# First MLP group's weights in GpSimd's queue, the last mixing product in another PSUM bank, and two tiles of activation sums exchanged

## The chip, the cores and the metric

The kernel runs on one core of one Trainium2 chip. A core has five engines, each with its own list of instructions that it works off in order: TensorE (PE in the profile; its weight loads are PEld), VectorE (DVE), ScalarE (ACT), GpSimd (POOL) and SyncE (SP). Engines wait for one another, and for transfers, by semaphores. Transfers are issued on a queue of the engine that issues them; here SP's queue is q1 in the profile and GpSimd's is q0, and 16 DMA engines carry both. The metric is device time in microseconds, the median of the runs shown.

## What is computed

A layer of a decoder with 512 tokens and width 2048, all in float32. The parts of the reference that matter here:

```python
merged = gc * conv_branch + ga * attn_branch
x = x + jnp.einsum('bsd,de->bse', merged, w_mix_out[l])

h = rmsnorm(x, g_mlp[l])
u = jnp.square(jax.nn.relu(jnp.einsum('bsd,df->bsf', h, w_ff1[l])))   # 2048 -> 8192
x = x + jnp.einsum('bsf,fd->bsd', u, w_ff2[l])                        # 8192 -> 2048
```

The three products are called mixing, FF1 and FF2 below.

## The kernel before

**Seven products for eight.** Every large product is cut in two along the tokens, the inner dimension and the output columns, and the eight quarter products are made from seven (the Winograd form of Strassen's scheme). A group makes 512 output columns. The seven activation operands are called A11, A12, A22 (quarters) and S1, S2, S3, S4 (sums and differences of quarters). Of the weights there are four quarters X[i, j], the tiles x00, x10, x01, x11 of 1024 KB each, 128 partitions by 8 runs of 256 floats; S1 takes x01 - x00, S2 takes x11 less that, S3 takes x11 - x01, A22 takes x10 less what S2 took. VectorE makes these differences (line 113). The profile leaves the numbers out: tile x is a weight quarter, A and S are operands.

**Three float32 passes.** TensorE multiplies rounded parts. Each weight tile is split into a high part th (ScalarE, line 103) and a rest tl (VectorE, line 104), each activation operand likewise, and a product is hi*hi + hi*lo + lo*hi: 48 matmuls of 256 columns, first the 32 that need th, then the 16 that need tl (in mixing, in two halves by token block, each with 16 and 8). Line 172, 173 and 175 are these three in mixing and FF2, lines 153, 155 and 157 in FF1; an `extra` in front (line 146) is one matmul of 192 columns. There are two buffers of th and of tl.

**Sums in PSUM.** A group adds its products in four PSUM banks a, b, c, d. ScalarE copies a bank into a tile o (`snap`, line 233), VectorE adds another bank to it (`plus`, line 116), and `put` hands a finished quarter of the output on.

**From mixing to the MLP.** Mixing has four groups g = 0 to 3, each a `Group` whose head runs A11 and A12 and whose tail runs the rest; the last uses `tail3` with the order S1, S2, S4, S3, A22. `Mix.put` adds the residual x (line 1111), stores the quarter into x1_d (line 1112) and leaves a `turn` in the list `waiting`. A turn squares the quarter for the norm (line 464), turns it by four TensorE transposes into a bank ptr (line 1128) and lets ScalarE write it with the gain into f (line 1137); the last group writes columns of Q2's A11 and A12 straight from ptr (lines 1133, 1134). From the two f tiles of a mixing group VectorE makes the sums s1, S2, S3, S4 of the next operand set Q2 (`first_of`, `sums`), and `give` splits them and sends them to h_d in HBM (line 1153). Shortly before FF1 the first three quarters of each Q2 operand come back from f_d (A11, A12; 768 KB, line 1088) and h_d (the others; 1536 KB each in runs of 6 KB, line 1086), all on GpSimd's queue, and the last mixing group adds the last quarter on chip (`mix.out`).

**Where the order comes from.** `Steps` attaches work to the moment after a product's matmuls have been written down, by the product's name: turns, `begin_part` (a load of a Q2 operand), `split_part` (A11's and A12's loaded columns). A scheduler then orders each engine's list by what it expects to be ready, except for instructions pinned with `keep_in_program_order` or `issue_after`. Weight tiles sit in four slots x0 to x3, handed out from the list `free`; a load waits for the last use of its slot's former tile. All weight quarters are loaded on SP's queue (line 208). The first MLP group g0 loads x00 and x10 in `head`, x01 in `first_sum`, x11 in `tail2`.

**From FF1 to FF2.** FF1's 16 groups store the activation sums of FF2 in s_d. For each of 8 segments `load_sums` brings them into four tiles us in slots t4, t1, t3, t2 by the table US (line 1331, 1 MB per transfer of two operands, GpSimd's queue). For the first segment these slots hold Q2 operands of FF1's last group: t1 holds S1, t3 holds S3, t4 A12, t2 A22. That group runs S4, S2, S3, S1, A22, so t3 falls free a product before t1. FF2's weights are the tiles y.

Of the kernel before, what the change touches and what calls it, by code (L numbers as in the profile page):

```python
# [45 lines left out]
def tile_hybrid_block(ctx: ExitStack, tc, x, g_mix, w_in, b_f, b_gate, conv_w, w_conv_out,  # L46
# [143 lines left out]
    class Group:  # L190
# [3 lines left out]
        def __init__(self, view, c1, c2, w, ST, mm, banks, put, scale=1.0, extra={}, after=None, shift=SHIFT):  # L194
# [3 lines left out]
            self.begun = False  # L198
# [3 lines left out]
        def load(self, i, j):  # L202
# [5 lines left out]
            nc.sync.dma_start(out=t, in_=src[i])  # L208
# [45 lines left out]

        def first(self):

            self.X = {}
# [6 lines left out]
        def head(self, keep=False, between=lambda: None, order=((0, 0), (1, 0)), rows=lambda i: None):  # L264
# [4 lines left out]
            else:  # L269
                X = self.X = {}  # L270
                for i, ij in enumerate(order):
                    X[ij] = self.load(*ij)
                    rows(i)
# [51 lines left out]
        def first_sum(self, pinned=True):  # L325

            self.pinned = True
            X = self.X
            X[0, 1] = self.load(0, 1)
# [41 lines left out]
        def tail3(self):  # L371
# [24 lines left out]
            self.run(d, "A22", X[1, 0], False)  # L396
            self.done(1, 0)
            self.plus(s2, d)
# [792 lines left out]
    before = None  # L1191
    mixes, groups = {}, []
    for g in range(4):
        def put_mix(i, j, v, g=g):
            mixes[g].put(i, j, v)

        banks = ((2,), (7,), (0,), (1,)) if g == 0 else steady(g)
        groups.append(Group(w_mix_out, g * S, g * S + HS, HS, M.moving, mm_rows if g else mm_late, banks, put_mix,
                            shift=48))
    for g in range(4):  # L1200
        mix = mixes[g] = Mix(g)
        after = Steps()
        if g == 0:
            for n, n2 in zip(("A11", "A12", "S1", "S3", "S2"), ("S1", "S3", "S2", "S4", "A22")):
                after.add(n, quads3[n2])
        if g == 3:
            after.add("S1", mix.fourth, lambda: begin_part("A12", 4))
        late = g == 1
        for n in ("A12", "S3") if late else ("A11", "S1"):
            after.add(n, turn_waiting)  # L1210
        after.add("A22", turn_first)
        if before:
            after.add("A12" if late else "A11", before.first_of, before.sums)
            for n, part in (("A12", "S1"), ("S1", "S3"), ("S2", "A22")):
                after.add(n, lambda before=before, part=part: before.give(part))
        if g < 3:
            after.add("S2", mix.fourth)
        else:
            after.add("A12", lambda: begin_part("A11", 0))
            after.add("S4", lambda: begin_part("S1", 1))  # L1220
# [5 lines left out]
        if g == 0:  # L1226
            after.add("A11", group.first_sum)
# [29 lines left out]

    held = []

    def put_u(g):
# [301 lines left out]
```

## Time and profile before

| | us |
|---|---|
| runs | 2448.61, 2451.72, 2453.45 |
| median | 2451.72 |
| the profiled execution | 2450.91 |
| its span, first to last instruction | 2449.2 |
| mixing's last group and the first MLP group | about 1156 to 1252 |
| FF1 ends, FF2 begins | 1825.3 |

In the timeline a row is a start, a duration, the engine, the line, the operation, and output<-input; brackets give the engine's idle time before the row and what ended it. A TensorE row's duration holds the pipeline's tail, so consecutive starts tell its pace better than durations.

### The profile page before, as it was taken

The page shows a single profiled execution, that of the slowest core. Times are in us where ns is not written, and L with a number is a line of the kernel's source. Part 1 is how long each engine was busy: PE and PEld are TensorE (multiplying, and loading weights), DVE is VectorE, ACT ScalarE, POOL GpSimd, SP SyncE. Part 2 cuts the span into 40 slices and gives each one's busy share as a digit, 9 for nine tenths or more (in the row PEclk, how much of TensorE's full clock was granted, in tenths as well). Part 3 has the DMA queues.
Part 4 walks back from the last instruction along what each step waited for, and adds up shares of the span by engine and source line. Part 5 has one row for each costly group of instructions (what it writes and reads, how often), then busy time and mean ns, then how long its engine had stood idle before and what let it go on. Part 6 is the DMA issues. An engine that isn't in the chain of part 4 may idle for free.

```text
span 2449.2 us, 41518 instructions
## 1 busy us (share of the span) xinstructions
PE 2409.1 (98%) x17800; PEld 2265.7 (93%) x17800; DVE 2041.6 (83%) x1717; ACT 1203.6 (49%) x1233; POOL 275.8 (11%) x442
## 2 busy tenths in 40 slices
PE   8999999999999999999899999999999999999998
PEld 8999899999999999899899999999997888888886
DVE  7987777788887778888889898898978888889898
ACT  6443434345455535356556666666655333333334
POOL 0100000111121111022300000000011001100000
PEclk9999999999999999999999999999999999999999
DMA  7664544454656655657854655646587476655662
GB/s 250 184 192 143 155 132 145 138 161 164 211 171 214 217 196 179 215 161 246 309 181 176 228 194 200 236 176 229 198 304 271 167 246 228 236 191 183 245 225 101
DMA packets 286988, 489.87 MB, mean 200 GB/s; under 512 B 11772, under 2 KB 199284, under 8 KB 286420
## 3 DMA queue, kind: packets, MB, share of 16 engines
q1 hardware_dynamic: 237072, 283.20, 36.6%
q0 software_dynamic: 48864, 202.92, 22.3%
q8 instruction: 139, 2.28, 0.4%
q10 hardware_dynamic: 868, 1.10, 0.1%
q14 instruction: 45, 0.37, 0.0%
HBM read 377.60 MB, written 109.05 MB: 199 GB/s over the span
## 4 chain that ended last, share of the span: by engine, by line
PE 90%; DVE 4%; DMA 3%; issue 2%; ACT 1%; POOL 1%; SPq 0%; DVEq 0%; POOLq 0%; ACTq 0%
PE a L157 6%; PE a L153 6%; PE a L155 6%; PE a L173 5%; PE a L175 5%; PE a L172 5%; PE d L153 5%; PE d L155 5%; PE d L157 5%; PE c L153 4%; PE c L155 4%; PE c L157 4%; PE d L172 3%; PE d L175 3%; PE d L173 3%; PE b L155 3%
## 5 line engine op out<-in xcount | busy, mean ns | idle before, releaser
L103 ACT ACTIVATE th<-x 128x2048 fp32r<-128x2048 f32 (+1 forms) x280 | 537.0, 1918 | 509.2 <-DVE x L113 169.5
L104 DVE TENSOR_TENSOR tl<-x,th 128x2048 fp32r<-128x2048 f32 (+1 forms) x280 | 638.8, 2286 | 166.6 <-ACT th L103 151.6
L113 DVE TENSOR_TENSOR x<-x,x 128x2048 f32<-128x2048 f32 (+1 forms) x160 | 365.6, 2285 | 28.6 <-DMA x<-in_w_in_dram 16.9
L103 ACT ACTIVATE th<-y 128x2048 fp32r<-128x2048 f32 (+1 forms) x109 | 185.4, 1701 | 273.1 <-PE a L173 138.8
L104 DVE TENSOR_TENSOR tl<-y,th 128x2048 fp32r<-128x2048 f32 (+1 forms) x109 | 218.9, 2013 | 28.9 <-ACT th L103 28.4
L172 PE MATMUL a<-th,us 128*128 128x512 f32 x512 | 199.9, 390 | 2.2 <-ACT th L103 2.2
L153 PE MATMUL c<-S,th 128*128 128x256 f32 x848 | 197.6, 278 | 2.5 <-ACT th L103 2.5
L173 PE MATMUL a<-th,us 128*128 128x512 f32 x512 | 199.8, 390 | 0.0
L155 PE MATMUL c<-S,th 128*128 128x256 f32 x848 | 197.0, 277 | 0.0
L153 PE MATMUL a<-S,th 128*128 128x256 f32 x784 | 182.6, 278 | 0.8 <-ACT th L103 0.8
L155 PE MATMUL a<-S,th 128*128 128x256 f32 x784 | 181.1, 276 | 0.0
L153 PEld LDWEIGHTS c<-S,th 128*128 128x128 f32 x848 | 159.8, 188 | 3.0 <-ACT th L103 2.7
L155 PEld LDWEIGHTS c<-S,th 128*128 128x128 f32 x848 | 159.7, 188 | 0.0
L153 PEld LDWEIGHTS a<-S,th 128*128 128x128 f32 x784 | 147.3, 188 | 1.0 <-ACT th L103 1.0
L155 PEld LDWEIGHTS a<-S,th 128*128 128x128 f32 x784 | 147.3, 188 | 0.0
L175 PE MATMUL a<-tl,us 128*128 128x512 f32 x512 | 137.5, 391 | 0.0
L155 PE MATMUL b<-A,th 128*128 128x256 f32 x544 | 128.4, 280 | 0.4 <-DVE A L104 0.4
L153 PE MATMUL b<-A,th 128*128 128x256 f32 x544 | 128.2, 280 | 0.0
L153 PE MATMUL d<-S,th 128*128 128x256 f32 x544 | 126.3, 278 | 0.0
L153 PE MATMUL a<-A,th 128*128 128x256 f32 x544 | 126.1, 277 | 0.0
L155 PE MATMUL a<-A,th 128*128 128x256 f32 x544 | 126.0, 277 | 0.0
L155 PE MATMUL d<-S,th 128*128 128x256 f32 x544 | 125.8, 277 | 0.0
(386 smaller groups left out, 6058.7 us busy)
## 6 DMA issues: line engine op xcount, KB each, us to landing
x<-in_w_in_dram SPq DMA_DIRECT2D x86, 1024.0 KB, 6.0
x<-in_w_ff_dram SPq DMA_DIRECT2D x64, 1024.0 KB, 8.4
y<-in_w_ff_dram SPq DMA_DIRECT2D x64, 1024.0 KB, 7.8
us<-s_d POOLq DMA_DIRECT2D x48, 1024.0 KB, 9.2
s_d<-rh POOLq DMA_DIRECT2D x32, 896.0 KB, 5.5
s_d<-r POOLq DMA_DIRECT2D x32, 896.0 KB, 6.1
x<-in_w_mix_out_dram SPq DMA_DIRECT2D x17, 1024.0 KB, 6.7
g_d<-o POOLq DMA_DIRECT2D x32, 256.0 KB, 3.0
```

The costliest lines, as they stand in the source:

```text
L103: a = nc.scalar.activation(out=hi, in_=src, func=AF.Copy, scale=one)
L104: b = nc.vector.tensor_tensor(out=lo, in0=src, in1=hi.bitcast(F32), op=ALU.subtract)
L113: return nc.vector.tensor_tensor(out=out, in0=a, in1=b, op=ALU.subtract)
L153: nc.tensor.matmul(o, hi[:, q, js], Sh, start=first and q == 0 and j == 0, stop=False, skip_group_check=True)
L155: nc.tensor.matmul(o, hi[:, q, js], Sl, start=False, stop=False, skip_group_check=True)
L157: nc.tensor.matmul(o, lo[:, q, js], Sh, start=False, stop=q == nq - 1, skip_group_check=True)
L172: nc.tensor.matmul(o, Sh, hi[:, q, :], start=begin and q == 0, stop=False, skip_group_check=True)
L173: nc.tensor.matmul(o, Sl, hi[:, q, :], start=False, stop=False, skip_group_check=True)
L175: nc.tensor.matmul(o, Sh, lo[:, q, :], start=False, stop=q == nq - 1, skip_group_check=True)
```

## The change

Three edits. First, `Group` gets a queue, and g0's is GpSimd's; the four quarters of g0 are loaded by a new method `ahead`, which is attached to the last mixing group's steps S4 (x00), S3 (x10) and A22 (x01) and to g0's own A11 (x11). `head`, `first_sum` and `tail2` then load only what is not there yet. For this the setup of the mixing groups moves, unchanged otherwise, behind the definition of `put_u`, `ff1` and g0. Second, in `tail3` the last product A22 starts anew in bank a instead of adding to d; d is added to s2 before, by a `plus` of its own. With it the turns of the last group that waited behind S1 wait behind S2. Third, in US the slots of (S2, S3) and (S1, A22) are exchanged.

```diff
-            self.begun = False
+            self.begun, self.queue, self.X = False, nc.sync, {}
...
-            nc.sync.dma_start(out=t, in_=src[i])
+            self.queue.dma_start(out=t, in_=src[i])
...
+        def ahead(self, i, j):
+
+            self.X[i, j] = self.load(i, j)
+
...
         def first(self):
 
-            self.X = {}
             self.X[0, 0] = self.load(0, 0)
...
-                X = self.X = {}
+                X = self.X
                 for i, ij in enumerate(order):
-                    X[ij] = self.load(*ij)
+                    if ij not in self.at:
+                        X[ij] = self.load(*ij)
                     rows(i)
...
         def first_sum(self, pinned=True):
 
             self.pinned = True
-            X = self.X
-            X[0, 1] = self.load(0, 1)
+            X = self.quarters((0, 1))
             one = sub(X[0, 0], X[0, 1], X[0, 0])
...
             self.put(1, 1, d1)
-            self.run(d, "A22", X[1, 0], False)
+            self.plus(s2, d)
+            self.run(a, "A22", X[1, 0], True)
             self.done(1, 0)
-            self.plus(s2, d)
+            self.plus(s2, a)
             self.put(1, 0, s2)
...
     g0 = ff1(0, ((5,), (0,), (1,), (7,)))
-    g0.after = Steps(A11=[turn_waiting, begin_rest, lambda: first_sum_after(mix.added), mix.first_of],
+    g0.queue = nc.gpsimd
...
+        for n in ("A12", "S3") if late else ("A11", "S2" if g == 3 else "S1"):
             after.add(n, turn_waiting)
...
             after.add("A12", lambda: begin_part("A11", 0))
-            after.add("S4", lambda: begin_part("S1", 1))
+            after.add("S4", lambda: g0.ahead(0, 0), lambda: begin_part("S1", 1))
             after.add("S4", lambda: split_part("A11"))
-            after.add("S3", lambda: begin_part("S3", 3))
+            after.add("S3", lambda: g0.ahead(1, 0), lambda: begin_part("S3", 3))
+            after.add("A22", lambda: g0.ahead(0, 1))
             after.add("A22", lambda: split_part("A12"))
...
+    g0.after = Steps(A11=[lambda: g0.ahead(1, 1), turn_waiting, begin_rest, lambda: first_sum_after(mix.added), mix.first_of],
                      A12=[lambda: mix.out("S1", mix.s1), mix.sums, lambda: factors(common, turned)])
...
-    US = ((4, ("A11", "A12")), (1, ("S2", "S3")), (3, ("S1", "A22")), (2, ("S4",)))
+    US = ((4, ("A11", "A12")), (3, ("S2", "S3")), (1, ("S1", "A22")), (2, ("S4",)))
```

The scheduler orders the engines' lists anew around these places. GpSimd's list from the last store of a rest into h_d to the load of A22, before (numbers behind a name are the program's own for a buffer):

```order
L1153 DMA h_d_76<-f_11978 128x512 x2
L1086 DMA S1_12831<-h_d_76 128x2x1536
L1112 DMA x1_d_78<-o_12836 128x2x256
L1086 DMA S3_12894<-h_d_76 128x2x1536
L1112 DMA x1_d_78<-o_12716 128x2x256
L1112 DMA x1_d_78<-o_12776 128x2x256
L1086 DMA S2_13052<-h_d_76 128x2x1536
L1086 DMA S4_13054<-h_d_76 128x2x1536
L1086 DMA A22_13056<-h_d_76 128x2x1536
```

and now:

```order
L208 DMA x00_12833<-in_w_ff1_dram 128x8x256
L208 DMA x10_12898<-in_w_ff1_dram 128x8x256
L1157 DMA h_d_76<-staged_12772 128x512
L1157 DMA h_d_76<-f_11980 128x512
L1090 DMA S1_12835<-h_d_76 128x2x1536
L1116 DMA x1_d_78<-o_12840 128x2x256
L1090 DMA S3_12900<-h_d_76 128x2x1536
L1116 DMA x1_d_78<-o_12703 128x2x256
L208 DMA x01_12984<-in_w_ff1_dram 128x8x256
L1116 DMA x1_d_78<-o_12778 128x2x256
L208 DMA x11_13044<-in_w_ff1_dram 128x8x256
L1090 DMA S2_13057<-h_d_76 128x2x1536
```

x00 and x10 stand ahead of the second staged pair (a high part and its rest) and of S1, x01 before the last store, x11 behind it and ahead of S2, S4 and A22.

TensorE at the end of S1 (bank c) in the last mixing group, before:

```order
L175 MATMUL c_12638<-tl_12640,M_10796 128x256 x2
L175 MATMUL c_12638<-tl_12640,M_10996 128x256 x2
L1128 MATMUL ptr_12699<-ident_90,o_12564 128x128 x4
L172 MATMUL a_12472<-th_12718,M_10549 128x256
L173 MATMUL a_12472<-th_12718,M_10549 128x256
```

and now at the end of S2 (bank a):

```order
L175 MATMUL a_12474<-tl_12706,M_10796 128x256 x2
L175 MATMUL a_12474<-tl_12706,M_10996 128x256 x2
L1132 MATMUL ptr_12761<-ident_90,o_12566 128x128 x4
L173 MATMUL c_12640<-th_12781,M_10549 128x256
L172 MATMUL c_12640<-th_12781,M_10549 128x256
```

The four transposes (in one row) moved from the start of S2 to its end; one matmul of S4 now stands in front of S2's first tl.

VectorE behind the last mixing store and around the first MLP group's S1 (x00 becomes x01 - x00, s1 is made from the last turn, S1 and A22 are the rests of split operands), before:

```order
L113 TENSOR_TENSOR x00_12984<-x01_13058,x00_12984 128x2048
L104 TENSOR_TENSOR tl_13067<-x10_12986,th_13066 128x2048
L104 TENSOR_TENSOR A12_12693<-A12_12693 128x1536
L1245 TENSOR_REDUCE ms_13124<-ss2_11038 128x4
L104 TENSOR_TENSOR tl_13156<-x00_12984,th_13155 128x2048
L116 TENSOR_TENSOR s1_13061<-f_12465 128x512
L104 TENSOR_TENSOR A22_13056<-f_12465,A22_13056 128x512
L113 TENSOR_TENSOR f_12465<-f_12464,f_12465 128x512
L104 TENSOR_TENSOR S1_12831<-s1_13061,S1_12831 128x512
L113 TENSOR_TENSOR f_12464<-s1_13061,f_12464 128x512
```

and now:

```order
L104 TENSOR_TENSOR A22_13061<-f_12467,A22_13061 128x512
L113 TENSOR_TENSOR x00_12833<-x01_12984,x00_12833 128x2048
L104 TENSOR_TENSOR S1_12835<-s1_13064,S1_12835 128x512
L113 TENSOR_TENSOR f_12467<-f_12466,f_12467 128x512
L113 TENSOR_TENSOR f_12466<-s1_13064,f_12466 128x512
L1310 TENSOR_REDUCE mean_13134<-mean_13132 128x1
L113 TENSOR_TENSOR f_12466<-f_12466 128x512
L116 TENSOR_TENSOR o_13066<-b_13068,o_13066 128x512
L104 TENSOR_TENSOR S3_12900<-f_12467,S3_12900 128x512
L104 TENSOR_TENSOR S2_13057<-f_12466,S2_13057 128x512
L104 TENSOR_TENSOR S4_13059<-f_12466,S4_13059 128x512
L104 TENSOR_TENSOR tl_13157<-x00_12833,th_13156 128x2048
```

The difference x01 - x00 moved behind s1 (now one row ahead of the piece) and A22's rest, and the split of its result moved from in front of s1 to behind the rests of S3, S2 and S4.

117 lines of the change are left out of this document (58 added, 59 removed).

## The prediction

> **What bounds the kernel now.** The page's head comes first.
>
> ```profile
> span 2449.2 us, 41518 instructions
> PE 2409.1 (98%) x17800; PEld 2265.7 (93%) x17800; DVE 2041.6 (83%) x1717; ACT 1203.6 (49%) x1233; POOL 275.8 (11%) x442
> ```
>
> TensorE stands still for 40.1 us of the span. Only such gaps, and slow stretches behind them, can be won. I then listed TensorE in order of time around the two places that the diff touches. First the seam from mixing to the MLP (in brackets: idle time before the row, and what ended it):
>
> ```profile
> 1174.91 0.63 PE L1128 MATMUL ptr<-ident,o 128*128 128x128 f32 x4 [0.78 <-DVE o L1111]
> ...
> 1178.22 1.18 PE L175 MATMUL a<-tl,M 128*128 128x256 f32 x8 [0.86 <-DVE tl L104]
> ...
> 1193.88 0.36 PE L172 MATMUL d<-th,M 128*128 128x256 f32 x1 [0.88 <-DVE o L116]
> ...
> 1205.78 0.60 PE L1128 MATMUL ptr<-ident,o 128*128 128x128 f32 x4
> 1209.15 0.36 PE L146 MATMUL b<-A,th 128*128 128x192 f32 x1 [2.78 <-ACT A L103]
> ...
> 1212.19 0.58 PE L153 MATMUL c<-S,th 128*128 128x256 f32 x1 [2.54 <-ACT th L103]
> ...
> 1238.58 2.05 PE L157 MATMUL a<-S,tl 128*128 128x256 f32 x16
> ```
>
> The two long waits open the first MLP group's A12 and S1. The windows (TensorE's busy time first; the last three figures are granted clock, DMA share and GB/s) show a second price behind them:
>
> ```profile
> 1209.00:1212.00 3.00, 0.49 (x2) 0.30 (x2) 3.00 (x2) 2.27 (x4) 0.00 (x0) 0.93 1.02 402
> 1212.00:1215.00 3.00, 2.38 (x9) 2.09 (x10) 3.00 (x4) 2.26 (x7) 0.81 (x1) 0.50 1.03 411
> ```
>
> From 1212 the clock is halved, and the DMA engines are full at some 400 GB/s. Now the engines TensorE waited for:
>
> ```profile
> 1203.57 1.92 ACT L103 ACTIVATE th<-x 128x2048 fp32r<-128x2048 f32 x1 [4.73 <-DMA x<-in_w_ff_dram]
> ```
>
> ```profile
> 1207.84 2.29 DVE L113 TENSOR_TENSOR x<-x,x 128x2048 f32<-128x2048 f32 x1 [6.34 <-DMA x<-in_w_ff_dram]
> ...
> 1214.02 2.28 DVE L104 TENSOR_TENSOR tl<-x,th 128x2048 fp32r<-128x2048 f32 x1
> 1216.22 0.68 DVE L116 TENSOR_TENSOR s<-f 128x512 f32<-128x512 f32 x1
> 1216.82 0.68 DVE L104 TENSOR_TENSOR A<-f,A 128x512 fp32r<-128x512 f32 x1
> ```
>
> ScalarE stood 4.73 us until weight quarter x10 had landed, with A12's operand split queued behind, which is the ACT A that ended the 2.78; VectorE stood 6.34 us for x01. So at this seam the bound is the landing of two weight quarters. Why they are late: the DMA view gives the issues from 1178 to 1212 (size, median us to landing), and the queues from 1194 to 1196 (packets, MB, share of 16 engines):
>
> ```profile
> x<-in_w_ff_dram SPq DMA_DIRECT2D x4, 1024.0 KB, 22.1
> ```
>
> ```profile
> q0 software_dynamic: 112, 0.69, 84.2%
> q1 hardware_dynamic: 113, 0.11, 16.2%
> ```
>
> SP's queue (q1) and GpSimd's (q0) get equal packets, but a packet of an operand load is 6 KB and one of a weight quarter 1 KB. The weights get 0.11 MB of each 0.80 and take 22.1 us.
>
> **The change part by part.** *Weights in GpSimd's queue.* One queue serves its loads in the order of issue, so x00 and x10 no longer share with S1 and S3, and x01 follows S3. When do they land? GpSimd's queue is empty of older work by about this issue:
>
> ```profile
> 1179.78 0.54 POOL L1088 DMA_DIRECT2D A<-f_d  x1
> ```
>
> From there (sizes from the code) x10 ends a list of 1.83 MB of older transfers (four of 0.26 and A12's load, 0.79) and 2.10 MB of weights: 9.8 us at 400 GB/s, 1190. x01 has 9.16 MB up to its end (those 3.93, the staged pair 0.52, S1 and S3 3.15, two stores 0.52, itself 1.05): 22.9 us, 1203; with up to 2 us until the semaphore, 1205. Four issues more on GpSimd; the nearest row is
>
> ```profile
> L1331 POOL DMA_DIRECT2D us<-s_d x64 | 47.9, 752 | 369.8 <-PE b L175 218.0 <-PE d L175 105.1 <-PE a L175 26.9
> ```
>
> 0.75 us for 512 runs of 2 KB. A quarter has 1024 runs of 1 KB; between 0.75 and twice that I take 0.8, 3.2 us in all on an engine 11% busy. Behind x00 stand the second staged pair and S1, behind x01 a store and x11: all have microseconds to spare. SP loses four issues that nobody waits for.
>
> *A22 in bank a.* The 0.88 us before 1193.88 goes: bank a was read out before S3. The price is one more VectorE addition, 0.60 us (start to start of the 0.68 rows above), between additions that wait for S3 anyway: nothing.
>
> *Transposes after S2 instead of S1.* S2 still waits for tl, which VectorE makes at the same time:
>
> ```profile
> 1175.89 2.28 DVE L104 TENSOR_TENSOR tl<-x,th 128x2048 fp32r<-128x2048 f32 x1
> ```
>
> So S2 begins at 1174.0, where the wait before the transposes of 1174.91 began, runs its first 16 matmuls, stands until 1178.2 and ends as before; the four transposes, which lay in idle time, now cost about 0.4. Together with the line above, A11 starts 0.9 - 0.2 = 0.7 earlier, if tl holds S2 exactly as now.
>
> *The new path behind A11.* A11 ends near 1204.9, transposes 1205.2. A12's hi and lo parts are made by then, since x10 is there by 1192 and ScalarE's buffer free by 1198, so A12 runs 1205.6 to 1211.1 without its 2.78. The last turn's copies on ScalarE end at 1206.2. From there VectorE's new list is followed at 0.60 for 512 columns and 2.20 for 2048 (starts of the three rows from 1214.02): s1, A22's lo (1207.5), x01-x00 (1209.7), S1's lo and two sums (1211.5), then mean, which needs A12's end, five of 512 (1214.7), S1's tl (1216.9), S3's difference (1219.1), S3's tl after ScalarE's 1.9 (1223.2), S2's difference (1225.4). TensorE: S1 from 1211.6, its 32 hi matmuls 3.6 us, then 1.6 idle for tl, end 1218.8; S3 from 1221.0 (2.2 idle) to 1226.5; S2 from 1227.4 to 1232.9. Before, S2 ended at 1238.58 + 1.9 = 1240.5. **The sum is -7.6 us**, about VectorE's 6.34 us plus the 0.7; S4 and all after it are paced by TensorE (the chain of waits, the last part of each product):
>
> ```profile
> 1267.01 1.88 PE c L157 x16
> 1272.66 1.81 PE a L157 x16
> 1278.10 1.81 PE d L157 x16
> ```
>
> A product takes 5.65 us up to 1268 and 5.44 later. From 1240.5 five slow ones may become fast: 0 to -1.05; I take 0, as new gaps lie ahead of them too.
>
> *Places of S2,S3 and S1,A22 swapped.* At the seam from FF1 to FF2:
>
> ```profile
> 1814.91 1.52 POOL L1331 DMA_DIRECT2D us<-s_d  x2 [0.48 <-PE d L157]
> 1820.35 1.49 POOL L1331 DMA_DIRECT2D us<-s_d  x2 [3.92 <-PE a L157]
> ```
>
> ```profile
> 1834.32 2.29 DVE L113 TENSOR_TENSOR t<-y,y 128x2048 f32<-128x2048 f32 x1 [1.14 <-DMA y<-in_w_ff_dram]
> ```
>
> ```profile
> 1838.67 0.50 PE L172 MATMUL a<-th,us 128*128 128x512 f32 x1 [2.20 <-ACT th L103]
> ```
>
> ```profile
> us<-s_d POOLq DMA_DIRECT2D x2, 1024.0 KB, 15.4
> ```
>
> The tile freed first (1814.91) now takes S2,S3, 5.4 us earlier. But the pair issued at 1820.35 had landed, 15.4 us by the median, near 1837, before 1838.67; what came last was the weight difference t, begun at 1834.32. Same bytes, same issue times: 0. If the sums were the bound instead, up to -2.2.
>
> **The rivals.** *Half clock in the new gaps.* S2 of the last mixing group now stands 2.3 us in one piece, and S3 2.2. For the price there is
>
> ```profile
> 1838.00:1843.00 5.00, 4.33 (x12) 3.17 (x13) 5.00 (x3) 4.49 (x4) 0.56 (x1) 0.66 0.34 137
> ```
>
> after the single gap of 2.20: a third of 5 us, 1.7. Against it: the window behind the 2.78 gap shows 0.93, and 0.50 came only after a second gap. At S2 it costs 1.7, at S3 0.8, since 0.9 lies in S2's wait: -5.9 to -5.1, 2445.8 to 2446.6. [...]
>
> *The queue changes nothing.* The engines were full anyway, and x01 lands as late as now; left are the 0.7: 2451.0. For it: the same bytes must move from 1180 on. Against it: 22.1 us came from the 0.11 of 0.80 MB, and what is loaded ahead instead (S2, S4, A22) is needed later. [...]
>
> *Slower: the queue starves S1.* S1, S3, x00, x10 and nine smaller transfers now stand ahead of x01 in one queue, much of it in runs of 1 KB. From 1182 to 1184, when almost only weight packets moved, the answer was
>
> ```profile
> DMA packets 438, 0.47 MB, mean 237 GB/s; under 512 B 2, under 2 KB 429, under 8 KB 438
> ```
>
> At 237 GB/s the 9.16 MB take 38.6 us; x01 is there at 1220.6, 13.1 after VectorE wants it (1207.5): 13.1 - 7.6 = +5.5, 2457.2. It decides from 277 GB/s downward. Against it stand later 2 us of almost nothing but weights:
>
> ```profile
> q1 hardware_dynamic: 718, 0.72, 106.8%
> ```
>
> that is 360 GB/s. *Partly late*: at 320 GB/s x01 is 3.1 late, -4.5, 2447.2. [...]
>
> **How the numbers follow.** The profiled run took 2450.91 us, 1.7 more than its span, and lies 0.8 under the median of three, 2451.72. With -7.6 on the median: 2444.1. Chances: forecast 0.50, half clock 0.15, partly late 0.13, queue without effect 0.11, starved 0.11. The likeliest's own range is 2441.5 to 2446.5. The whole: down to -7.6 - 1.05 - 1.7 (no half clock at the second seam) = -10.4, taken as 2440.8, up to 2451.5, past the case without effect. What a measurement can tell is 0.2%, 4.9 us: faster below 2446.8, slower above 2456.6. Faster: nearly all of the forecast, most of the half clock, a third of the partly late: 0.65; slower 0.10; same 0.25.
>
> **What would show it.** ScalarE's th<-x for x10 and VectorE's x01-x00 without a DMA behind them; A12 within 0.5 us of the transposes; idle times of some 1.6, 2.2 and 0.9 before S1's tl, S3 and S2; no gap before A22; S2's end at the second seam unmoved against the landing of y. Wrong it would be if x01 still ends VectorE's wait, if weights in q0 take over 10 us from their turn, or if S2 of the last mixing group ends later than now.

## The result, and the profile after

| | before | changed |
|---|---|---|
| median of the runs compared, us | 2453.72 (20 runs, 2448.31 to 2459.63) | 2445.68 (20 runs, 2440.90 to 2449.22) |
| ratio, 95% interval | | 0.9964 (0.9956 to 0.9973) |
| the profiled execution, us | 2450.91 | 2446.44 |

The change makes the kernel 0.36% faster, 8.8 us by the ratio (6.6 to 10.8). The two profiled executions differ by 4.5 us only: the one of before lies 2.8 us under the median of its kernel, the one of the change 0.8 above its own.

The head of the page of the changed kernel:

```profile
span 2444.7 us, 41518 instructions
PE 2408.0 (98%) x17800; PEld 2265.2 (93%) x17800; DVE 2042.6 (84%) x1718; ACT 1203.9 (49%) x1233; POOL 277.9 (11%) x446
```

TensorE stands for 36.7 us of the span, before 40.1. Its timeline at the first seam (start, duration, engine, line, operation; in brackets the idle time and what ended it), from the last mixing group's S2 on:

```profile
1178.16 0.39 PE L172 MATMUL c<-th,M 128*128 128x256 f32 x1 [2.23 <-ACT o L233]
...
1193.37 0.28 PE L172 MATMUL a<-th,M 128*128 128x256 f32 x1
...
1205.17 0.60 PE L1132 MATMUL ptr<-ident,o 128*128 128x128 f32 x4
...
1212.29 0.39 PE L153 MATMUL c<-S,th 128*128 128x256 f32 x1 [0.60 <-ACT th L103]
...
1217.61 2.15 PE L157 MATMUL c<-S,tl 128*128 128x256 f32 x16 [1.41 <-DVE tl L104]
1221.81 0.53 PE L146 MATMUL d<-S,th 128*128 128x192 f32 x1 [2.05 <-ACT th L103]
...
1232.94 2.05 PE L157 MATMUL a<-S,tl 128*128 128x256 f32 x16
```

A22 follows at 1193.37 without a gap; A12 follows the transposes of 1205.17 without the 2.78 us. S2 stands 2.23 us in one piece. S1 and S3 of the first MLP group come within 0.8 us of the forecast, up to 1221.81, and S2's last part starts at 1232.94 where before it started at 1238.58. ScalarE and VectorE on the way there:

```profile
1192.66 1.92 ACT L103 ACTIVATE th<-x 128x2048 fp32r<-128x2048 f32 x1 [0.97 <-PE d L173]
...
1198.57 1.92 ACT L103 ACTIVATE th<-x 128x2048 fp32r<-128x2048 f32 x1
```

```profile
1206.73 0.69 DVE L116 TENSOR_TENSOR s<-f 128x512 f32<-128x512 f32 x1 [0.72 <-ACT f L1141]
...
1208.01 2.28 DVE L113 TENSOR_TENSOR x<-x,x 128x2048 f32<-128x2048 f32 x1
...
1215.27 2.28 DVE L104 TENSOR_TENSOR tl<-x,th 128x2048 fp32r<-128x2048 f32 x1
1217.47 2.29 DVE L113 TENSOR_TENSOR x<-x,x 128x2048 f32<-128x2048 f32 x1
1221.79 2.29 DVE L104 TENSOR_TENSOR tl<-x,th 128x2048 fp32r<-128x2048 f32 x1 [2.04 <-ACT th L103]
```

Neither th of x10 (1198.57) nor x01-x00 (1208.01) has a transfer behind it now. From 1206.73 VectorE works without a pause until 1219.76, and S1's tl and S3's difference are the end of that list: VectorE has taken the place of the transfers. The windows here are laid on the grid on which the granted clock changes (TensorE's busy time first, the granted clock third from the end):

```profile
1214.88:1218.29 3.41, 2.00 (x17) 1.81 (x16) 3.41 (x3) 0.00 (x0) 0.00 (x0) 1.00 1.03 422
1218.29:1221.71 3.42, 1.47 (x13) 1.26 (x11) 1.47 (x1) 1.86 (x2) 0.00 (x0) 1.00 0.70 286
1221.71:1225.12 3.41, 3.31 (x15) 3.31 (x16) 3.33 (x3) 1.29 (x3) 0.00 (x0) 0.50 0.04 14
```

One stretch of 3.41 us at half clock (from 1221.71) follows S3's wait of 2.05 us and costs 1.7 us. Before there were two at this seam (6.83 us from 1211.5) and one at the second seam; there the changed kernel has none. In the DMA view from 1178 to 1212 the weights now read:

```profile
q0 software_dynamic: 2808, 11.98, 95.8%
...
x<-in_w_ff_dram POOLq DMA_DIRECT2D x4, 1024.0 KB, 10.2
```

That is 10.2 us from issue to landing instead of 22.1. The figure alone says little: x01 was issued 12.5 us later than before (1198.10 against 1185.65) and landed at the same time.

### The profile page after: what moved, and what is told of

Same layout as the page of the kernel before. It is cut to its first block, busy times and chain, and to the rows that moved or that the text cites. A ratio compares the mean times of both kernels' runs of the same rounds, so it can differ in the third digit from the quotient of the medians.

```text
span 2444.7 us, 41518 instructions
## 1 busy us (share of the span) xinstructions
PE 2408.0 (98%) x17800; PEld 2265.2 (93%) x17800; DVE 2042.6 (84%) x1718; ACT 1203.9 (49%) x1233; POOL 277.9 (11%) x446
## 4 chain that ended last, share of the span: by engine, by line
PE 90%; DVE 4%; issue 2%; DMA 2%; ACT 1%; POOL 1%; SPq 0%; DVEq 0%; POOLq 0%; ACTq 0%
PE a L157 6%; PE a L153 6%; PE a L155 6%; PE a L175 5%; PE a L173 5%; PE a L172 5%; PE d L153 5%; PE d L155 5%; PE d L157 5%; PE c L153 4%; PE c L155 4%; PE c L157 4%; PE d L175 3%; PE d L173 3%; PE d L172 3%; PE b L153 3%
## 5 line engine op out<-in xcount | busy, mean ns | idle before, releaser
L113 DVE TENSOR_TENSOR x<-x,x 128x2048 f32<-128x2048 f32 (+1 forms) x160 | 366.1, 2288 | 21.2 <-DMA x<-in_w_in_dram 17.1
```

Source lines behind the costliest of these rows:

```text
L113: return nc.vector.tensor_tensor(out=out, in0=a, in1=b, op=ALU.subtract)
```

## The experiments

Each kernel was timed beside the kernel before on the same chip; a ratio's interval is turned into us at 2453 us. Places are counted from the start of the last mixing group's S1, since that start shifts by up to 4.0 us from one profile to the next (1168.04 to 1172.01). A product's end is counted as the start of the next one.

**The parts by themselves.** First the queue alone: the changed kernel with these three places put back.

```diff
+            self.run(d, "A22", X[1, 0], False)
+            self.done(1, 0)
             self.plus(s2, d)
-            self.run(a, "A22", X[1, 0], True)
-            self.done(1, 0)
-            self.plus(s2, a)
...
-        for n in ("A12", "S3") if late else ("A11", "S2" if g == 3 else "S1"):
+        for n in ("A12", "S3") if late else ("A11", "S1"):
...
-    US = ((4, ("A11", "A12")), (3, ("S2", "S3")), (1, ("S1", "A22")), (2, ("S4",)))
+    US = ((4, ("A11", "A12")), (1, ("S2", "S3")), (3, ("S1", "A22")), (2, ("S4",)))
```

> The first edit alone: the weights of the first MLP group in GpSimd's queue; the last mixing product stays in bank d, the turns stay behind S1, the places of the sums stay as they were. Theory (all of the gain comes from the first edit, the others together give at most 0.7 us): -7 us against before, between -5.5 and -8.5, and the end of the first MLP group's S2 near 1235.5 where before has 1240.5 and the whole change 1234.8. Rival (bank, turns and exchanged sums carry a part): -5 us or less.

Measured: ratio 0.9975 (0.9961 to 0.9989), -6.1 us (-9.6 to -2.7); S2 ended at 1236.08. The figure lies in the range of the theory, but the interval holds the rival's -5 as well. In the profile the queue alone carries 4 of the 5.6 us at this seam. It still shows 1.45 and 1.30 us of waits in A12, because in this list x10's load stood behind S1's and landed at 1200.7.

The other two edits, each alone on the kernel before:

```diff
-            self.run(d, "A22", X[1, 0], False)
+            self.plus(s2, d)
+            self.run(a, "A22", X[1, 0], True)
             self.done(1, 0)
-            self.plus(s2, d)
+            self.plus(s2, a)
...
-        for n in ("A12", "S3") if late else ("A11", "S1"):
+        for n in ("A12", "S3") if late else ("A11", "S2" if g == 3 else "S1"):
```

> The second edit alone: the last mixing product in bank a, and the turns of the last mixing group behind S2. Theory: the gap before A22 goes, S2 keeps its stall, TensorE's idle time from the last mixing group's S1 to the end of the first MLP group's S2 falls from 10.2 to about 9.3 us; at most -1 us against before, apart from half-clock stretches. Rival (the bank or the turns carry the 4 us by which the run with loads on SP lay under before): -3 us or more.

```diff
-    US = ((4, ("A11", "A12")), (1, ("S2", "S3")), (3, ("S1", "A22")), (2, ("S4",)))
+    US = ((4, ("A11", "A12")), (3, ("S2", "S3")), (1, ("S1", "A22")), (2, ("S4",)))
```

> The third edit alone: the places of (S2, S3) and (S1, A22) exchanged. Theory: 0 within the error, TensorE's wait for S2 at the second seam stays between 0.8 and 2.7 us and ends with the weight difference, not with the sums. Rival (the sums were the bound): -2.2 us, and no wait there.

Measured: bank and turns 0.9986 (0.9975 to 0.9998), -3.4 us (-6.1 to -0.5); the exchanged sums 1.0000 (0.9988 to 1.0011). So the exchange is worth nothing, as forecast; S2 of the second seam waited 1.67 us for th there, behind a weight difference that had waited 1.15 for y. Bank and turns are worth something; the interval holds the forecast 0.7 near its edge, and the -3.4 itself is the rival's figure. Both profiles were a surprise. VectorE and TensorE of the kernel with bank and turns alone, at the first seam:

```profile
1213.90 2.29 DVE L113 TENSOR_TENSOR x<-x,x 128x2048 f32<-128x2048 f32 x1 [11.26 <-DMA x<-in_w_ff_dram]
```

```profile
1218.25 0.58 PE L153 MATMUL c<-S,th 128*128 128x256 f32 x1 [10.50 <-ACT th L103]
```

With the weights still on SP's queue x01 came 4 us later than in the first profile of before, and TensorE stood 10.5 us in one piece. The two edits touch neither the queue nor the issue of that load (17.1 us behind S1's start in both). Idle time from S1 to S2's end was 15.2 us, not the expected 9.3. The same profile shows what bank and turns are worth beyond the forecast: x10 landed 6.2 us earlier than before, and the wait of 2.78 us before A12 is gone. With the turns behind S2, GpSimd issued no transfer between 13.3 and 20.2 us behind S1's start, where before it issued four stores from 16.2 on and S1's load at 19.8.

Then everything but the queue:

```diff
-    g0.queue = nc.gpsimd
```

> The whole change, but the four weight quarters stay on SP's queue; their loads are written at the new places. So it holds the second and the third edit without the first. VectorE's list keeps x01-x00 ahead of A12's rest, as before. Theory (the second and third edit give next to nothing): -0.4 us against before, between -1.0 and +0.3; A11 starts some 0.6 earlier, ScalarE again stands some 4 to 5 us for x10, VectorE some 6 us for x01, S2 of the first MLP group ends near 1240. Rival (writing the loads earlier is what counts, or the exchanged sums): -3 us or more.

Measured: 0.9983 (0.9967 to 1.0), -4.2 us (-8.1 to 0), with runs from 2441.65 to 2461.26. That is the rival's figure, not the theory's, though the interval reaches 0. x10 and x01 came early in its profile (1195.94, 1206.96), so ScalarE did not stand for x10, VectorE stood 3.58 us for x01 and S2 ended at 1240.53. Here too the scatter is larger than what was to be measured.

**Queue or list?** x01 landed at 1207.81 before and at 1207.79 after: in that pair the queue had not brought it forward. What had changed as well is VectorE's list: before, x01-x00 stands ahead of A12's rest, s1 and the sums, afterwards behind. The next two kernels are meant to separate the two. The list of the change with SP's queue:

```diff
-    g0.queue = nc.gpsimd
...
-            add(self.s1, self.F[1][:, 0], self.F[1][:, 1])
+            self.s1_add = nc.vector.tensor_tensor(out=self.s1, in0=self.F[1][:, 0], in1=self.F[1][:, 1], op=ALU.add)
...
-    g0.after = Steps(A11=[lambda: g0.ahead(1, 1), turn_waiting, begin_rest, lambda: first_sum_after(mix.added), mix.first_of],
+    g0.after = Steps(A11=[lambda: g0.ahead(1, 1), turn_waiting, begin_rest, mix.first_of, lambda: first_sum_after(mix.s1_add)],
```

> As the run with all loads on SP, but VectorE's difference x01-x00 is put behind s1 in its list, where the change has it, so that it no longer stands in front of A12's rest. The landings stay those of SP's queue: x10 near 1203.5, x01 near 1207.8. In the changed kernel x01 landed at 1207.79, in the kernel before at 1207.81, so the queue brought only x10 and x11 earlier. Theory of the landing (x10's 8.5 us earlier are what pays): A12 still waits for x10 and its operand split on ScalarE, -2 us or less against before, S2's end at 1238 or later. Rival, theory of the list (what paid is that VectorE does A12's rest, s1 and the sums while x01 is still on its way): A12 near 1211 to 1217, S3's th near 1221, S2's end near 1235, -4.5 to -6 us against before.

And GpSimd's queue with the old list (`behind` stands for a dependency of order only):

```diff
-            split(src, hi, lo)
+            rest = split(src, hi, lo)[1]
+            if n == "A12" and self.queue is nc.gpsimd:
+                behind(rest, self.one)
...
-            one = sub(X[0, 0], X[0, 1], X[0, 0])
+            one = self.one = sub(X[0, 0], X[0, 1], X[0, 0])
...
-            add(self.s1, self.F[1][:, 0], self.F[1][:, 1])
+            ins = nc.vector.tensor_tensor(out=self.s1, in0=self.F[1][:, 0], in1=self.F[1][:, 1], op=ALU.add)
+            if self.last:
+                behind(ins, g0.one)
```

> The whole change with GpSimd's queue, but in VectorE's list s1 and A12's rest are held behind x01-x00, as in the kernel before. x01 lands near 1207.8, x10 near 1195. Theory of the landing: A12 starts at 1205.5 and stands some 3 us before its tl, yet most of the gain stays, -5 us against before. Theory of the list: VectorE stands until 1207.8 and has some 5 us of work behind that in the change was done before or meanwhile; S1's rest begins near 1218 to 1220 where the change has 1215.3, S2's end 2.5 to 4 us later than the change's 1234.8, -1.5 to -4 us against before.

Measured: the list of the change on SP's queue 0.9989 (0.9976 to 1.0002), -2.7 us (-5.9 to +0.5), and S2 ended at 1239.82; the queue with the old list 0.9978 (0.9967 to 0.9989), -5.4 us (-8.1 to -2.7), S2's end 2.9 us later than in the change when counted from S1. On SP's queue with that list TensorE's two waits read:

```profile
1214.32 0.38 PE L153 MATMUL c<-S,th 128*128 128x256 f32 x1 [2.76 <-ACT th L103]
1225.97 0.53 PE L146 MATMUL d<-S,th 128*128 128x192 f32 x1 [4.32 <-ACT th L103]
```

and VectorE's reasons for them:

```profile
1210.03 2.29 DVE L113 TENSOR_TENSOR x<-x,x 128x2048 f32<-128x2048 f32 x1 [2.73 <-DMA x<-in_w_ff_dram]
...
1221.63 2.29 DVE L113 TENSOR_TENSOR x<-x,x 128x2048 f32<-128x2048 f32 x1 [1.35 <-DMA x<-in_w_ff_dram]
```

Where the list no longer stands in the way, S1 waits for x01 and S3 for x11 (landed at 1221.60; 1212.24 in the change). So the theory of the list fell: S2's end and the time miss what it expected, and the interval includes 0. A premise of that run did not hold either: x10 landed at 1194.86 on SP's queue too, not near 1203.5, and A12 did not wait. This bought little: S4 ended 76.26 us behind S1, before at 77.59 and 76.46. The theory of the landing got its -5 us for the queue with the old list, but not the profile: S1's rest began at 1220.51 and S2's end came as late as the list's theory had it. By the profiles the change needs both: its S4 ends at 72.0 and 72.5 us behind S1, that of the queue with the old list at 74.8, that of the list on SP's queue at 76.3, that of neither at 75.0. The runs give -8.8 us for both, -5.4 for the queue alone, -2.7 for the list alone and -4.2 for neither (everything but the queue, above); the last three intervals overlap, and these times do not separate the queue from the list. All four kernels hold the other two edits as well.

**The same kernels again.**

> The kernel before once more, for a second profile of it. Theory (with the weights on SP's queue the landings of x10 and x01 scatter from one execution to the next, and the first profile of before was an early one): x01 lands anywhere between 36 and 45 us behind the start of the last mixing group's S1 (39.3 in the first profile), and the later it lands the longer TensorE stands and the more half-clock stretches follow. Rival (the first profile is typical, the landing fixed): 39.3 within 0.5, idle time from that S1 to the end of the first MLP group's S2 10.2 within 0.5. On the clock: in all profiles so far a stretch of 3.41 us in which TensorE stood for 1.88 us or more was followed by one at half clock, and one with at most 1.76 was not; the same is expected here.

> The changed kernel once more, for a second profile of it. Theory (one queue serves in order, so the landings hardly scatter): x01 lands 38.9 to 40.1 us behind the start of the last mixing group's S1, as in the three profiles with GpSimd's queue, idle time to the end of S2 6 to 7 us, the time -6 to -10 us against before. Rival: x01's landing moves by 3 us or more here too.

Measured: before against itself 1.0003 (0.9987 to 1.0019); the change 0.9971 (0.9959 to 0.9984). The profiles so far together (us behind the start of the last mixing group's S1; idle is TensorE's, to the end of the first MLP group's S2; half-clock stretches and the last column to the end of S4):

| kernel | x10 lands | x01 lands | idle | half-clock stretches | S4 ends |
|---|---|---|---|---|---|
| before | 34.95 | 39.28 | 10.18 | 2 | 77.59 |
| before, again | 34.87 | 39.54 | 10.28 | 2 | 76.46 |
| sums exchanged alone | 33.46 | 44.43 | 14.95 | 4 | 82.52 |
| bank and turns alone | 28.71 | 43.50 | 15.20 | 4 | 81.48 |
| all but the queue | 24.94 | 35.96 | 9.32 | 1 | 74.97 |
| SP's queue, new list | 25.86 | 41.01 | 8.85 | 3 | 76.26 |
| GpSimd's queue, old list | 25.07 | 38.90 | 7.79 | 2 | 74.83 |
| queue alone | 32.66 | 40.05 | 6.81 | 2 | 73.48 |
| the change | 26.46 | 39.28 | 6.29 | 1 | 71.96 |
| the change, again | 26.50 | 39.92 | 6.96 | 1 | 72.47 |

The second profile of before, taken by itself, came out as the rival had it: x01 at 39.54, within 0.5 of 39.28, and the idle time at 10.28. What speaks for the scatter is the kernel with the exchanged sums alone. Its code is that of before except for a table used at the second seam, and its x01, issued at the same place, landed at 44.43. Over all six profiles with SP's queue x01 lands from 36.0 to 44.4, over the four with GpSimd's from 38.9 to 40.1; these are profiles of five and three kernels.

x10's landing does not follow the queue. It is early, 24.9 to 28.7, in all kernels in which the turns wait behind S2, with either queue, and late, 32.7 to 35.0, in all in which they wait behind S1. What follows the queue is x11: it lands 52.6 to 54.6 us behind S1 in the six profiles with SP's queue and 42.4 to 43.7 in the four with GpSimd's. In the change VectorE begins S3's difference, which needs x11, 49.0 us behind S1, before x11 would have landed on SP's queue.

The two profiles of before have times in the lower half of their kernel's: 2450.91 and 2448.03, where 12 runs of it have a median of 2454.30. Between them and the two of the change the seam, to S4's end, shrinks by 4.8 us on average (77.0 to 72.2). Over the five profiles with SP's queue and the old list it takes 78.6 us, 6.4 more than in the change, but three of these are of other kernels. The granted clock that every run lists shows another part. It averages 0.9960 over 78 runs of before and 0.9979 over 29 of the change; (1 - clock) times 2450 us is 9.7 and 5.2 us lost. By that estimate about half of the 8.8 us is half-clock time that no longer arises, and the rest would be waits that are gone.

**The next bound.** In the change VectorE's list runs from 1206.73 to 1219.76 without a pause. First only x01 earlier: its load ahead of S3's operand, and x01-x00 right behind A12's rest.

```diff
             self.done(0, 1)
+            self.freed()
...
-            after.add("S3", lambda: g0.ahead(1, 0), lambda: begin_part("S3", 3))
-            after.add("A22", lambda: g0.ahead(0, 1))
+            after.add("S3", lambda: g0.ahead(1, 0))
...
+        group.freed = lambda: (g0.ahead(0, 1), begin_part("S3", 3))
...
-    g0.after = Steps(A11=[lambda: g0.ahead(1, 1), turn_waiting, begin_rest, lambda: first_sum_after(mix.added), mix.first_of],
+    g0.after = Steps(A11=[lambda: g0.ahead(1, 1), turn_waiting, begin_rest, lambda: first_sum_after(part_rest["A12"]), mix.first_of],
```

`part_rest["A12"]` is the instruction on VectorE that makes the rest of A12's loaded columns.

> The whole change, with x01's load issued as soon as its slot is free, ahead of the load of S3's operand, and x01-x00 put right behind A12's operand rest on VectorE. Theory (behind A12 VectorE's own list is the bound, not the landing any more): x01 lands near 1203.3 instead of 1207.8, VectorE does x01-x00 from about 1206, and S3's difference x11-x01 ends 1.0 to 1.5 us earlier than in the changed kernel, because tl of S1 still stands behind the rests of S3, S2, S4; S2's end some 1.2 us earlier, the time -1 to -2 us against the changed kernel. Rival (the landing of x01 is still the bound): -4 us or more against the changed kernel.

Then, on top, S1's rest and S3's difference ahead of the operand rests of S3, S2, S4 and A22:

```diff
+            self.third(third)
...
-            sub(X[two], X[1, 1], X[0, 0])
+            self.two(sub(X[two], X[1, 1], X[0, 0]))
...
-    for n in SPLIT[1:]:
-        mix.out(n, mix.parts[n])
+    def rest_of(ins, *names):
+        with tc.issue_after(ins.ins):
+            for n in names:
+                mix.out(n, mix.parts[n])
...
+    g0.third = lambda ins: rest_of(ins, "S3")
+    g0.two = behind
```

with `behind` calling `rest_of` for S2, S4 and A22.

> As the run with x01's load early, and on VectorE the rest of S1's weights and S3's weight difference go ahead of the operand rests of S3, S2, S4 and A22. Theory (VectorE's list is the bound behind A12): TensorE's gaps before S1's tl, S3 and S2 shrink from 2.0, 2.05 and 0 (with a half-clock stretch of 1.7 between) to 0, at most 0.5 and some 0.9, none long enough for the clock to halve; S2 ends near 1230.5 on a run that starts the last mixing group's S1 at 1168.5, 66.3 us behind it in the changed kernel, 62 here; -4 to -6 us against the changed kernel, -11 to -14 against before. Rival (the landings or TensorE's pace bound it): no more than -2 us against the changed kernel.

> The kernel with x01's load early and the operand rests late once more, beside the changed kernel in the same turn. Theory (VectorE's list was the next bound): 3 to 6 us below the changed kernel, x01 34 to 36 us behind the last mixing group's S1, idle time to the end of S2 4.0 to 4.6 us. Rival (the first six runs of it were lucky): less than 2 us below the changed kernel.

Measured: x01 early alone 0.9951 (0.9936 to 0.9967), median 2441.24; with the rests late 0.9947 (0.9931 to 0.9964), 2441.64, and again 0.9950 (0.9937 to 0.9963), 2440.66 beside 2446.53 of the change, timed with it. The second kernel's gaps behind the last mixing group, all of them, from its first profile:

```profile
1219.95 0.35 PE L147 MATMUL d<-S,th 128*128 128x192 f32 x1 [1.07 <-ACT th L103]
1226.63 0.38 PE L154 MATMUL a<-S,th 128*128 128x256 f32 x1 [0.84 <-ACT th L103]
```

S1 has none, where the change had 2.0. No stretch at half clock is left at this seam or the next in either profile; the idle time is 3.60 and 3.67 us, somewhat below the expected 4.0 to 4.6, and S4 ends at 67.07 and 67.50 in place of 71.96. In the profiles, then, VectorE's list was the bound behind A12: with its order changed, the gaps it had made shrink. Both kernels beat the one before by 0.5% and the changed one by 4 to 6 us by the medians. The profile with x01 early alone (x01 36.1 us behind S1, idle 5.83, one half-clock stretch) gains only 0.9 us at the seam, about what was expected, S4 ending at 71.06 with a gap of 2.11 before S3. Yet its runs are as fast as those with the rests late: -4.4 us against the median of the change, the figure of its rival, by which x01's landing is still the bound. So the runs do not show what putting the rests late adds; they show the two steps together.

Last, S2 of the last mixing group with th for both token blocks ahead of tl, so that its 2.2 us are filled with work:

```diff
+            elif n in self.both:
+                mm_both(ps, self.ST(n), hi, lo, first)
...
+            group.both = ("S2",)
...
-            after.add("S4", lambda: g0.ahead(0, 0), lambda: begin_part("S1", 1))
+            after.add("S4", lambda: g0.ahead(0, 0))
...
+        group.freed4 = lambda: (g0.ahead(1, 0), begin_part("S1", 1))
```

`mm_both` is `mm_rows` with the loop over the parts outside that over the blocks.

The edit also moves loads: x10's was issued 19.0 us behind S1's start instead of 13.9.

> As that kernel, and in S2 of the last mixing group the matmuls that need th run for both token blocks before those that need tl; x10's load stays behind x00's. Theory: TensorE's stand of 2.2 us in that S2 shrinks to 0.3 to 0.6, and with it goes the stretch at half clock that followed it in 1 of 5 profiles with that stand; -1.8 to -2.5 us against the kernel without it, idle time to the end of the first MLP group's S2 2.3 to 2.8. Rival (S2's tl is late for another reason, or S4's tl comes later by as much): within 0.5 us of the kernel without it.

Measured: 0.9952 (0.9939 to 0.9964), 2441.07: no gain over the 2440.66, which is the rival's figure, though for a reason that it did not name. The stand is gone, and A11 starts 28.5 us behind S1 instead of 30.5, the 2 us as expected. But then A12 waits 0.88 us for its rest, VectorE waits for x11, and TensorE for VectorE:

```profile
1216.97 2.29 DVE L114 TENSOR_TENSOR x<-x,x 128x2048 f32<-128x2048 f32 x1 [0.94 <-DMA x<-in_w_ff_dram]
```

```profile
1221.32 0.36 PE L147 MATMUL d<-S,th 128*128 128x192 f32 x1 [2.10 <-ACT th L103]
```

```profile
1219.00:1222.41 3.41, 1.31 (x11) 1.11 (x11) 1.98 (x3) 1.91 (x1) 0.00 (x0) 1.00 1.00 411
1222.41:1225.83 3.42, 3.42 (x18) 3.42 (x18) 3.39 (x2) 0.00 (x0) 0.00 (x0) 0.50 0.60 240
```

The wait before S3 grows from 1.07 to 2.10 and brings a half-clock stretch of 1.7 us, while S2's 0.84 falls away: S4 ends 67.49 us behind S1, as without the edit (67.50). The expected gain became a wait for the last weight quarter, with 411 GB/s moving: the transfers are the bound again. Idle time to S2's end was 2.98 us, above the expected 2.3 to 2.8.

## Why the prediction was right, point by point

The forecast was 2444.1 us, -7.6 on the median of before; it came out at 2445.68, -8.0 by the medians of the comparison and -8.8 by the ratio. The mechanism holds: the waits for x10 and x01 are gone, and VectorE's list sets S1 and S3. The size came out partly by luck. In the profiled pair the seam gave -5.65, the figure of the half-clock rival (-5.9 to -5.1), and the runs gave 4.3 us more than the pair for reasons that are only in part shown (below).

- **x10 and A12: right in the effect, not in the cause.** x10 landed at 1194.97, 5 us later than the 1190 worked out, but nothing waited for it. A12 started at 1205.53 (forecast 1205.6) and ended at 1211.42 (1211.1). The forecast credited this to the queue. But with the queue alone x10 landed 32.7 us behind S1 and A12 waited 2.75 us, and with bank and turns alone, on SP's queue, x10 landed at 28.7 and A12 started without a wait. It is the second edit that brings x10 early; the forecast had given it 0.7 us of TensorE's time and nothing on the transfers.
- **x01: right in its effect, wrong in its time.** Forecast 1203 to 1205, landed 1207.79. The 9.16 MB from 1179.78 on went at 327 GB/s up to the landing, not at 400. No run shows the up to 2 us that the forecast allowed until the semaphore: in the profile of before a store of 256 KB that had the queues to itself (issued at 85.02) landed 2.5 us after its issue, and had no packet under way in its last 0.3 us. GpSimd's own list explains part of the lateness:

```profile
1191.55 0.73 POOL L1090 DMA_DIRECT2D S<-h_d  x1
1197.38 0.72 POOL L1116 DMA_DIRECT2D x_d<-o  x1 [5.10 <-issue]
1198.10 0.92 POOL L208 DMA_DIRECT2D x<-in_w_ff_dram  x1
```

  The load stood behind a store whose data VectorE finished at 1195.46 and which went out 1.9 us after that, so the load was issued 6.5 us after the load ahead of it. The lateness cost nothing: VectorE had no pause before x01-x00. It reached it at 1208.01 instead of 1207.5, because the last turn's copies on ScalarE ended at 1206.70 instead of 1206.2. The margin was 0.2 us, not the 2.5 to 4.5 of the forecast; that it sufficed was luck.
- **Issue on GpSimd: slightly low.** 0.92 us for a quarter (the row of 1198.10), estimated 0.8; nothing waited for it.
- **A22 in bank a: right.** The 0.88 us are gone, and A11 starts 0.6 us earlier behind S1 (forecast 0.7). For bank and turns together the runs give more than 0.7: -3.4 us alone (-6.1 to -0.5) and -4.2 with the third edit and loads written earlier (-8.1 to 0). Each interval still reaches 0.7; x10's earlier landing is a cause for more.
- **Transposes behind S2: right in the time, wrong in the wait.** S2 stood until 1178.16 (forecast 1178.2, when tl would be made). But tl was made 1.0 us earlier than before, and S2 stood for ScalarE's copy of bank c:

```profile
1174.88 2.29 DVE L104 TENSOR_TENSOR tl<-x,th 128x2048 fp32r<-128x2048 f32 x1
```

```profile
1177.53 0.58 ACT L233 ACTIVATE o<-c 128x512 f32<-128x512 f32 x1
```

  tl was ready at 1177.17. The scheduler had put one matmul of S4, which writes bank c anew, in front of S2's first tl; it had to wait for the copy, which ended at 1178.11, and S2's tl matmuls behind it. The second profile shows the same: tl ready at 1180.38, the matmul at 1181.40. So the forecast's 1178.2 was met by accident, and about 1 us was left there. The worry about the one-piece gap was justified: the first profile shows full clock behind it, the second not:

```profile
1178.10:1181.51 3.41, 1.15 (x11) 0.95 (x9) 2.90 (x4) 2.56 (x4) 1.87 (x4) 0.99 0.81 293
1181.51:1184.92 3.41, 3.41 (x16) 3.41 (x17) 3.41 (x4) 2.13 (x4) 2.77 (x6) 0.51 0.68 221
```

- **S1, S3, S2: right to 0.8 us, then the clock.** Idle times 2.0, 2.05 and 0 against 1.6, 2.2 and 0.9; S3 at 1221.81 against 1221.0. Then half clock behind S3's gap, which the forecast had as a rival and priced at 0.8: S2 ended at 1234.82, not 1232.9, and the seam gave -5.65 instead of -7.6 in this pair. VectorE's list needed x11 early for this, which the queue brought (1212.24, before 1222.95); the forecast did not name it.
- **Before, judged by one profile.** The sum was made from one profile of before. Its two half-clock stretches at the first seam were counted as they stood, and it was not foreseen that on SP's queue x01 can land 5 us later in another execution (44.43 us behind S1 with the sums exchanged alone, 39.28 in that profile). The runs exceed the pair, -8.8 against -4.5. About 1 us of that is half clock: the pair has three stretches inside the kernel before and one after, 3.4 us, where the mean clocks give 4.5 on average. About 1.5 us is pace (next point). The rest is not shown; longer waits of before in other executions are the likely cause, as in the profile of the exchanged sums alone.
- **Pace: 0 was right on average.** The products from S4 of the first MLP group to FF1's end took 586.4 us in the first profile of the change (13 of them at 5.65) and 583.8 in the second; before 584.9 and 583.8. Both kernels show both paces, so it is not the change's doing.
- **Exchanged sums: right.** Alone 1.0000. At the second seam S2 waited 2.04 us for th and 0.62 for tl, behind the weight difference t, which began at 1829.94 after 1.18 us of waiting for y.
- **Rivals.** *The queue changes nothing* was right on x01's landing in the profiled pair and wrong on the time: x11 lands about 10 us earlier in all four profiles with GpSimd's queue (42.4 to 43.7 us behind S1, against 52.6 to 54.6), and x01 within 1.2 us (38.9 to 40.1), where it scattered over 8.5 in six with the other queue (36.0 to 44.4). That x01 landed at the same time in the first pair was one draw. *Starved* did not come: the DMA engines moved 353 GB/s on average from 1178 to 1212, above the 277 from which it would have decided.

## What to carry to other kernels

Loads that are wanted in a known order landed in that order here when one queue carried them all (x00, x10, the operands of S1 and S3, x01 and x11 at 1192.05, 1194.97, 1199.96, 1204.37, 1207.79 and 1212.24, in the order of their issue); on a second queue the landing of one of them scattered by 5 us between profiles of the same instructions (x01 from 39.28 to 44.43 us behind S1), and a single profile showed only one draw of it. An edit that moves work between two steps also moves the transfers that hang on it: moving the turns brought a weight quarter 6.2 us earlier (x10, 28.71 us behind S1 instead of 34.95) on a queue that it did not touch. When a wait is taken away, write down the next engine's list up to the next product before counting the gain, and every wait that can end there, not only the one seen before: here the list was VectorE's, and an earlier load together with a new order of that list gave another 4 to 6 us. A stand of TensorE of 2.05 us cost nearly twice its length here, 1.7 us more: 1.96 us of it fell into one stretch of 3.41 us, and the granted clock of the next was 0.50.

## What was not expected of the hardware

**Half-clock stretches lay on a grid of 3.41 us, each behind a stretch with much idle time or at half clock.** In the middle of the program the granted clock fell to 0.50 for 3.41 us or a multiple of it: before from 1211.55 to 1218.38 and from 1839.60 to 1843.01, in the change from 1221.72 to 1225.13. Where one profile has two such falls, they lie a whole number of stretches apart (before 628.05 us or 184; the queue alone from 1207.81 and from 1224.88, 17.1 us or five). Laying that grid over each profile and taking TensorE's idle time in stretches at full clock, each of these was followed by a half-clock one:

| profile | stretch from | idle, us | clock of the next |
|---|---|---|---|
| before | 1208.13 | 2.93 | 0.50 |
| before | 1836.18 | 2.20 | 0.50 |
| before, again | 1206.61 | 2.92 | 0.50 |
| the change | 1218.30 | 1.96 | 0.50 |
| the change, again | 1178.10 | 2.26 | 0.51 |
| queue alone | 1204.40 | 2.39 | 0.50 |
| queue alone | 1221.46 | 1.89 | 0.50 |
| bank and turns alone | 1206.90 | 2.55 | 0.50 |
| both blocks | 1219.00 | 2.10 | 0.50 |

In the first profiles of before and of the change no other stretch at full clock from 1000 us to 2420 was; the largest idle times of those were 1.75 (before, from 1204.72) and 1.59 (the change, from 1832.70). A stretch already at half clock was followed by another with 1.07 us idle (before, from 1211.55). So in these profiles a gap of 2.0 to 2.7 us cost another 1.7 us, or nothing, by where it fell on the grid: at the second seam 2.20 us fell into one stretch before the change,

```profile
1836.15:1839.56 3.41, 1.21 (x6) 0.76 (x5) 3.41 (x4) 2.85 (x2) 0.00 (x0) 1.00 0.54 184
1839.56:1842.97 3.41, 3.41 (x10) 2.38 (x9) 3.41 (x2) 2.93 (x3) 0.56 (x1) 0.51 0.41 169
```

and 2.66 us were cut in three after it, 0.47, 1.57 and 0.62, of which the last two stretches are shown:

```profile
1832.72:1836.13 3.41, 1.84 (x8) 1.42 (x8) 3.41 (x2) 3.41 (x3) 0.01 (x1) 1.00 0.32 108
1836.13:1839.55 3.42, 2.80 (x13) 2.10 (x12) 3.42 (x3) 2.58 (x3) 0.90 (x2) 1.00 0.66 268
```

These figures are read off the profiles; no run varied the idle time by itself.

**A store issued late.** The store of 1197.38 above needs a quarter that VectorE had finished at 1195.46 (an addition of 0.68 us from 1194.78), 1.9 us earlier. What GpSimd waited for is not settled: a subtraction of 2.29 us ran on VectorE from 1195.37 to 1197.66, but the load of 1191.55 was issued in the midst of such a one (1190.79 to 1193.08).
